# A hybrid retention and attention layer on one core: the attention's values become the stationary operand, two heads side by side in the array

## The chip, the cores and the metric

The kernel runs on one core of one Trainium2 chip. The metric is device time in microseconds (us) for one execution of the whole program, as the median of several runs; lower is better. Lines are cited as L361, meaning line 361 of the kernel before; where the changed kernel's own number differs, this is said.

## The reference

One layer over 256 tokens of width 1024, all in float32. The part that the change touches is the mixer:

```python
h = rmsnorm(x, mix_norm_g[l])
proj = h @ w_in[l]
rq, rk, rv, rg, mq, mk, mv, ga, gb = jnp.split(proj, offsets, axis=-1)
...
ret = retention(rq, rk, to_heads(rv, RET_HEADS))
y_a = (from_heads(ret) * jax.nn.silu(rg)) @ ret_w_branch[l]
att = moba_attention(mq, mk, to_heads(mv, MOBA_HEADS), rel_bias)
y_b = from_heads(att) @ moba_w_branch[l]
merged = jax.nn.sigmoid(ga) * y_a + jax.nn.sigmoid(gb) * y_b
x = x + merged @ w_out[l]
h2 = rmsnorm(x, ffn_norm_g[l])
x = x + peer(h2, peer_w_q[l], peer_sub_keys[l], peer_u[l], peer_v[l])
```

With 256 tokens there is one attention block, so the attention is plain causal attention over 8 heads of 64 with a relative-position bias that is added before the softmax. The retention has 8 heads with keys of 64 and values of 128, in two chunks of 128 tokens: the first chunk's keys and values give a state (64x128 for each head) that the second chunk's queries read. `peer` is a retrieval over 16,384 experts and takes the larger part of the time; the change does not touch it.

## The kernel before, in words

**The mixer as a row of pieces.** Every projection is cut into units of 512 columns, and every unit into pieces of 256 rows of the weight (512 KB each). The main loop runs over 72 mixer pieces. For piece i it issues a load some pieces ahead (`load_to`), splits the weight of piece i+3 into a high and a low part (`cut`: ScalarE writes the high part at L147, VectorE the low one at L148), and multiplies piece i (`products`, 12 matmuls of 512 columns at L230 to L232, or 24 of 256 columns at L239 to L241). The high parts (`rhi`), the low parts (`rlo`) and the products' PSUM tiles (`acc`) are rings.

**Side work between the pieces.** Everything else is written as Python generators (`attention`, `retention`, the epilogues of the units, `biases`). After each piece `pump` advances up to three of them to their next `yield`. What a generator emits between two yields is put behind that piece on every engine's queue, so a `yield` more means one piece more between two steps. The schedule is manual: each engine executes its instructions in the order in which the code emits them, and waits on semaphores where an operand is not ready.

**The bias table.** `biases` multiplies the bias by a one-hot table (L822), writes the rows to DRAM (`skew`, L825, GpSimd's queue), and some yields later reads them back, shifted, in 8 DMAs (L833, GpSimd's queue) into `bias`.

**The attention.** `attention` runs over two blocks t of 128 queries. Scores for two heads at a time come from matmuls on the two row halves of the array (64 rows each, L361). VectorE adds the bias (L365), takes the maximum (L369), ScalarE takes the exponent and the sums (L371, 8 heads), VectorE the reciprocal of the sums (L375). Then, for each block kt of 128 keys, TensorE turns the probabilities `pr` of 8 heads (L383), ScalarE copies them to `prT` (L384), and TensorE multiplies with `prT` as the stationary operand and 64 columns of the values `mv` as the moving one (L389). The result has queries in the partitions. VectorE multiplies it by the reciprocal (L393, into `at`), TensorE turns it (L400), and `split_to` splits it into `ah` and `al`, which a later projection (`branch_b`) reads. t = 0 has one block of keys, t = 1 has two.

**The retention.** The state `kv` comes from matmuls of 128 columns of `kdec` (two heads) by 256 columns of `rv` (L416), of which two quarters are used. Scores are L428, the output L441, the state's part L446.

**Rotary.** The epilogue of units 0 and 512 (`rotary`) has VectorE multiply into `ra` and `rb_` (L320, L322), GpSimd add them (L324) and scale (L330), and TensorE turn the result (L273).

**Order.** `finish(att)` runs what is left of the attention ahead of the unit at column 5632, since that unit's output `sb` takes the place of `bias` in memory.

Of the kernel before, what the change touches and what calls it, by code (L numbers as in the profile page):

```python
# [19 lines left out]
OP = mybir.AluOpType  # L20
# [55 lines left out]
def layer_kernel(ctx, tc, x, mix_norm_g, w_in, ret_w_branch, moba_q_gain, moba_k_gain, moba_w_branch,  # L76
# [273 lines left out]
    def attention():  # L350
        ssum = wk.tile([P, NT, H], F32, name="ssum")
        for t in range(NT):
            w = (t + 1) * P
            pr = wk.tile([P, H, S], F32, name="pr")
            nh = 512 // w
            for i0 in range(0, 4, nh):
                ps = [side() for _ in range(2)]
                for j in range(nh):
                    for c in range(2):
                        b = slice(c * 64, (c + 1) * 64)  # L360
                        T.matmul(ps[c][:, j * w:(j + 1) * w], mqk[0][b, i0 + j, t * P:(t + 1) * P],  # L361
                                 mqk[1][b, i0 + j, :w], start=True, stop=True)
                for c in range(2):
                    n = slice(4 * c + i0, 4 * c + i0 + nh)
                    V.tensor_tensor(pr[:, n, :w], ps[c].rearrange("p (j k) -> p j k", j=nh),  # L365
                                    bias[:, n, S - w:], op=OP.add)
                    yield
            sm = wk.tile([P, H], F32, name="smx")
            V.tensor_reduce(sm, pr[:, :, :w], axis=AX.X, op=OP.max, negate=True)  # L369
            for h in range(H):  # L370
                A.activation(pr[:, h, :w], pr[:, h, :w], AF.Exp, bias=sm[:, h:h + 1], accum_out=ssum[:, t, h:h + 1])  # L371
                if h % 4 == 3:
                    yield
            rs = wk.tile([P, H], F32, name="rs")
            V.reciprocal(rs, ssum[:, t, :])  # L375
            yield
            po = side()
            for kt in range(t + 1):
                prT = t4([P, H, P], "prT")
                for q in range(2):  # L380
                    p = side()
                    for j in range(4):
                        T.transpose(p[:, j * P:(j + 1) * P], pr[:, 4 * q + j, kt * P:(kt + 1) * P], ident)  # L383
                    A.activation(prT[:, 4 * q:4 * q + 4, :], p.rearrange("p (j i) -> p j i", j=4), AF.Copy)  # L384
                yield
                yield
                for i in range(H):
                    h = 2 * (i % 4) + i // 4
                    T.matmul(po[:, h * 64:(h + 1) * 64], prT[:, i, :], mv[:, kt, h * 64:(h + 1) * 64],  # L389
                             start=(kt == 0 and i == 0), stop=(kt == t), skip_group_check=True)  # L390
            at = t2([P, 512], "at")
            for c in range(2):
                V.tensor_tensor(at.rearrange("p (i c d) -> p c i d", c=2, d=64)[:, c],  # L393
                                po.rearrange("p (i c d) -> p c i d", c=2, d=64)[:, c],
                                rs[:, 4 * c:4 * c + 4, None].to_broadcast([P, 4, 64]), op=OP.mult)
            yield
            yield
            p = side()
            for c in range(4):
                T.transpose(p[:, c * P:(c + 1) * P], at[:, c * P:(c + 1) * P], ident)  # L400
            split_to(ah[0][:, :, t * P:(t + 1) * P], al[0][:, :, t * P:(t + 1) * P],
                     p.rearrange("p (c q) -> p c q", c=4))
            yield

    def mv_epi(o):
# [3 lines left out]
        yield  # L409

    def retention():
        for q in range(2):
            p = side()
            for j in range(2):
                hp = 2 * q + j
                T.matmul(p[:, j * S:(j + 1) * S], kdec[:, hp * P:(hp + 1) * P], rv[0][:, hp * S:(hp + 1) * S],  # L416
                         start=True, stop=True)
            A.activation(kv[:, 2 * q:2 * q + 2, :], p.rearrange("p (j e) -> p j e", j=2), AF.Copy)
            yield
        for t in range(NT):  # L420
            s = slice(t * P, (t + 1) * P)

# [20 lines left out]
            for j in range(4 if t else 0):  # L443
                for c in range(2):
                    b = slice(c * 64, (c + 1) * 64)
                    T.matmul(os_[c][:, j * P:(j + 1) * P], rqdT[b, j, :], kv[b, j, c * P:(c + 1) * P], start=False,  # L446
                             stop=True, skip_group_check=True)
            for c in range(2):
                for j in range(4):
# [54 lines left out]
    def merge_gate(dst, j):  # L504
        def epi(o):
            if j == 0:
                for t in range(NT):
                    A.activation(by_token(dst)[:, t], o[t], AF.Sigmoid)
                return
# [144 lines left out]
    sb = ap.tile([P, KC, S], F32, name="sb", tag="b8d")  # L654
    unit(w0, KC, 4608, hx, "nat", merge_gate(sa, 0))
    unit(w0, KC, 5120, hx, "T", merge_gate(sa, 1))
    unit(w0, KC, 5632, hx, "nat", merge_gate(sb, 0), before=lambda: finish(att))
    unit(w0, KC, 2048, hx, "nat", swish(0))
    unit(w0, KC, 2560, hx, "nat", swish(1))
    unit(w0, KC, 6144, hx, "T", merge_gate(sb, 1))  # L660
# [154 lines left out]
    def biases():  # L815
# [9 lines left out]
        G.dma_start(skew.rearrange("p h j -> h p j"), rr[:, None, :].to_broadcast([H, SK, 384]))  # L825
        yield
        V.tensor_scalar(gain[:, 0:1], gain[:, 0:1], 0.125, None, op0=OP.mult)
        for _ in range(5):
            yield

        s_ = skew[:, :, :]
# [605 lines left out]
```

## Time and profile before

| | |
|---|---|
| median of 3 runs | 948.59 us (946.0 to 951.2) |
| the profiled execution | 945.74 us, of which the span of the profile is 944.0 us |
| TensorE (PE) | busy 935.0 us, 99% of the span |
| VectorE (DVE) | busy 792.2 us, 84% |
| ScalarE (ACT) | busy 522.7 us, 55% |
| GpSimd (POOL) | busy 395.7 us, 42% |
| the mixer's stretch, 0 to 243 us | PE 240.96, DVE 168.55, ACT 127.13, POOL 34.53 us busy |
| DMA | 320.40 MB, mean 339 GB/s |

How to read the lines below: a line of the timeline gives the start in us, the duration in us, the engine, the line of the kernel, the operation, output<-input by the program's names, sizes, the count of instructions merged in it, and in brackets the idle time of the engine just before with what ended it. Matmuls are pipelined, so a matmul's duration overlaps its successor's, and what counts is the distance between two starts. A float32 matmul shows as two records.

### The profile page before, as it was taken

What the parts mean: (1) busy time and instruction counts of PE and PEld (TensorE: products, weight loads), DVE (VectorE), ACT (ScalarE), POOL (GpSimd) and SP (SyncE); (2) the same over time, 40 slices, a digit from 0 to 9 for tenths busy, and PEclk for the clock granted to TensorE, in tenths of its full rate; (3) what the DMA queues carried; (4) which work ended last, traced back from release to release, by engine and by line L of the source; (5) the groups of instructions that cost most, each with busy time, mean ns of one, the idle gap of its engine ahead of it and who ended that gap; (6) DMA issues with size and microseconds to landing.
All of it is one profiled execution on the core that took longest, in us unless ns stands there. A gap on an engine that the chain in (4) does not pass through costs nothing.

```text
span 944.0 us, 19147 instructions
## 1 busy us (share of the span) xinstructions
PE 935.0 (99%) x7208; PEld 896.5 (95%) x7208; DVE 792.2 (84%) x1514; ACT 522.7 (55%) x958; POOL 395.7 (42%) x306
## 2 busy tenths in 40 slices
PE   9999999999999999999999999999999999999998
PEld 6887898998999999999999999999999999999997
DVE  6657557778678999999988999974989999898987
ACT  6554645544544445434678777876454545364553
POOL 3422010000203446534556776763547656564720
PEclk9999999999999999999999999999999999999999
DMA  9878779998798998999999999998999999999993
GB/s 321 235 193 237 236 205 298 304 300 261 248 371 327 405 396 280 404 407 364 408 357 392 379 375 376 375 407 318 385 360 401 409 383 407 373 397 400 405 360 117
DMA packets 109419, 320.40 MB, mean 339 GB/s; under 512 B 11373, under 2 KB 22518, under 8 KB 109199
## 3 DMA queue, kind: packets, MB, share of 16 engines
q1 hardware_dynamic: 64492, 184.43, 54.8%
q0 software_dynamic: 32512, 115.54, 32.4%
q10 hardware_dynamic: 12322, 19.21, 6.8%
q8 instruction: 57, 0.93, 0.4%
q14 instruction: 36, 0.29, 0.1%
HBM read 307.52 MB, written 13.14 MB: 340 GB/s over the span
## 4 chain that ended last, share of the span: by engine, by line
PE 74%; DVE 15%; DMA 7%; ACT 1%; issue 1%; POOL 1%; SPq 0%; DVEq 0%; POOLq 0%; ACTq 0%
PE acc L1284 13%; PE acc L1316 9%; PE side L1316 9%; PE acc L230 6%; PE side L737 6%; PE acc L231 6%; PE acc L232 6%; PE acc L1317 4%; PE side L1317 4%; DVE rows L1044 3%; DMA raw_ring<-in_peer_w_q_dram 2%; PE acc L239 2%; PE acc L241 2%; PE acc L240 2%; PE side L1314 2%; PE acc L1314 2%
## 5 line engine op out<-in xcount | busy, mean ns | idle before, releaser
L1033 POOL DMA_INDIRECT rows<-in_peer_u_dram,eg x86 | 108.5, 1262 | 72.9 <-DVE rows L1044 34.0
L1033 POOL DMA_INDIRECT rows<-in_peer_v_dram,eg x54 | 100.2, 1856 | 67.1 <-DVE vacc L1119 45.7
L737 PE MATMUL side<-ident,raw_ring 128*128 128x128 f32 x800 | 107.2, 277 | 0.0
L737 PEld LDWEIGHTS side<-ident,raw_ring 128*128 128x128 f32 x800 | 97.0, 192 | 0.0
L1161 ACT ACTIVATE oh_buf<-oh_more,tS 128x128 bf16<-128x128 f16 x176 | 58.6, 420 | 0.0
L1044 DVE SCALAR_TENSOR_TENSOR rows<-rows,h 128x1024 f32<-128x1024 f32 x43 | 52.4, 1232 | 4.1 <-DMA rows<-in_peer_u_dram,eg 4.1
L1119 DVE SCALAR_TENSOR_TENSOR vacc<-rows,av,vacc 128x1024 f32<-128x1024 f32 x43 | 55.1, 1281 | 0.1
L1256 ACT ACTIVATE cw<-W 128x352 fp32r<-128x352 f32 x58 | 28.6, 494 | 47.6 <-PE acc L1317 38.5
L1242 POOL TENSOR_TENSOR W<-W,gl 128x256 f32<-128x256 f32 (+20 forms) x32 | 27.5, 861 | 46.3 <-ACT gl L1241 39.5
L1257 DVE TENSOR_TENSOR cw<-W,cw 128x352 fp32r<-128x352 f32 x58 | 30.3, 522 | 18.0 <-ACT cw L1256 18.0
L580 POOL DMA_DIRECT2D x1d<-xt x1 | 0.7, 657 | 88.5 <-DVE xt L562 88.5
L1156 DVE TENSOR_TENSOR oh_more<-iota,tI 128x1024 f16<-128x1024 f16 x44 | 34.5, 785 | 0.0
L1157 DVE TENSOR_TENSOR oh_buf<-oh_more,tM 128x1024 f16<-128x1024 f16 x44 | 32.6, 740 | 2.2
L154 POOL TENSOR_TENSOR gny<-va,minus_half 128x8 f32<-128x8 f32 x2 | 4.3, 2126 | 66.7 <-DVE va L454 66.7
L1284 PE MATMUL acc<-hTd,raw_ring 128*128 128x128 f32 x256 | 31.2, 275 | 0.0
L1284 PEld LDWEIGHTS acc<-hTd,raw_ring 128*128 128x128 f32 x256 | 29.9, 192 | 0.0
L1211 PE MATMUL acc<-oh_buf 128*128 128x128 bf16 x176 | 24.4, 219 | 0.0
L1212 PE MATMUL acc<-oh_buf 128*128 128x128 bf16 x176 | 24.4, 219 | 0.0
L1225 ACT ACTIVATE W<-acc 128x512 f32<-128x512 f32 (+21 forms) x44 | 17.3, 394 | 10.9 <-PE acc L1212 8.5
L1227 DVE TENSOR_TENSOR W<-acc,W 128x264 f32<-128x264 f32 (+20 forms) x32 | 16.1, 502 | 6.5 <-ACT W L1225 5.3
L1244 ACT ACTIVATE W<-acc 128x256 f32<-128x256 f32 (+20 forms) x52 | 18.4, 353 | 4.4 <-PE acc L1284 4.4
L1211 PEld LDWEIGHTS <-oh_buf 128*128 128x128 f16 x176 | 19.8, 114 | 0.0
(2701 smaller groups left out, 3486.4 us busy)
## 6 DMA issues: line engine op xcount, KB each, us to landing
raw_ring<-in_peer_v_dram SPq DMA_DIRECT2D x128, 512.0 KB
raw_ring<-in_peer_u_dram SPq DMA_DIRECT2D x100, 512.0 KB
raw_ring<-in_w_in_dram SPq DMA_DIRECT2D x52, 512.0 KB
raw_ring<-in_peer_w_q_dram SPq DMA_DIRECT2D x16, 512.0 KB
raw_ring<-turned SPq DMA_DIRECT2D x16, 512.0 KB
W<-in_peer_u_dram SPq DMA_DIRECT2D x12, 512.0 KB
eraw<-in_peer_u_dram ACTq DMA_DIRECT2D x32, 128.0 KB
h<-in_peer_u_dram ACTq DMA_DIRECT2D x32, 128.0 KB
```

What stands on the lines that cost most here:

```text
L230: T.matmul(o[t], xh[:, s], wh, start=(k == 0), stop=False)
L231: T.matmul(o[t], xh[:, s], wl, start=False, stop=False)
L232: T.matmul(o[t], xl[:, s], wh, start=False, stop=(k == kc - 1))
L737: T.transpose(p[:, k * P:(k + 1) * P], r.rearrange("p (i k) -> p k i", k=KC)[:, 4 * q + k], ident)
L1033: G.indirect_dma_start(out=r, out_offset=None, in_=tab, in_offset=bass.IndirectOffsetOnAxis(ap=eg[:, j:j + 1], axis=0))
L1044: V.scalar_tensor_tensor(r, r, 1.0, h, op0=OP.mult, op1=OP.mult, accum_out=av[:, j:j + 1])
L1119: V.scalar_tensor_tensor(a, r, av[:, j:j + 1], a, op0=OP.mult, op1=OP.add)
L1161: A.activation(o1[:, j], hot[:, 0, :, j], AF.Copy, scale=tS[:, t, k + j:k + j + 1])
L1211: T.matmul(p[:, j * P:(j + 1) * P], hi, o1, start=True, stop=False)
L1284: T.matmul(pa[:, n:n + NA], uT[:, k * P:(k + 1) * P], hT[:, k], start=(c % 2 == 0 and k == 0), stop=(k == KC - 1), skip_group_check=True)
L1316: T.matmul(o[b][:, :2 * ND], vh[:, n], w, start=(c == 0), stop=False, skip_group_check=True)
L1317: T.matmul(o[b][:, :ND], vl[:, n], w[:, :ND], start=False, stop=(c == NK - 1), skip_group_check=True)
```

## The change

The change has five parts.

1. **The product with the values.** The operands change places: 64 columns of `mv` are stationary and 128 columns of `prT` moving. A head's result is 64 partitions by 128 queries, and the two heads of a pair are written to partitions 0 to 63 and 64 to 127 of the same PSUM tile, from the two column halves of the array (L396 in the changed kernel; 8 matmuls for each block of keys as before). The result comes out turned, so the turn at L400 and `at` are gone, and `split_to` reads the product's tile.
2. **The division by the sums.** Since queries now lie in the free dimension of the result, VectorE multiplies `pr` by the reciprocal ahead of the turns (L378 in the changed kernel), in two instructions with a yield between them, in place of L393 behind the product.
3. **More pieces ahead of the turns.** Behind that come 1 + 2t yields, where one stood before. For t = 0 the turns stand one piece later than before, for t = 1 three.
4. **The retention's state** comes from 8 matmuls of 64 columns of `kdec` by 128 columns of `rv`, in the two column halves as well, in one PSUM tile instead of two.
5. **The order of the rest.** The bias table is read three yields sooner, and `finish(att)` moves from ahead of the unit at column 5632 to its epilogue.

```diff
             rs = wk.tile([P, H], F32, name="rs")
             V.reciprocal(rs, ssum[:, t, :])
-            yield
+            for c in range(2):
+                n = slice(4 * c, 4 * c + 4)
+                V.tensor_tensor(pr[:, n, :w], pr[:, n, :w], rs[:, n, None].to_broadcast([P, 4, w]), op=OP.mult)
+                if not c:
+                    yield
+            for _ in range(1 + 2 * t):
+                yield
             po = side()
...
-                for i in range(H):
-                    h = 2 * (i % 4) + i // 4
-                    T.matmul(po[:, h * 64:(h + 1) * 64], prT[:, i, :], mv[:, kt, h * 64:(h + 1) * 64],
-                             start=(kt == 0 and i == 0), stop=(kt == t), skip_group_check=True)
-            at = t2([P, 512], "at")
-            for c in range(2):
-                V.tensor_tensor(at.rearrange("p (i c d) -> p c i d", c=2, d=64)[:, c],
-                                po.rearrange("p (i c d) -> p c i d", c=2, d=64)[:, c],
-                                rs[:, 4 * c:4 * c + 4, None].to_broadcast([P, 4, 64]), op=OP.mult)
-            yield
-            yield
-            p = side()
-            for c in range(4):
-                T.transpose(p[:, c * P:(c + 1) * P], at[:, c * P:(c + 1) * P], ident)
+                for i in range(4):
+                    for c in range(2):
+                        h = 2 * i + c
+                        T.matmul(po[c * 64:(c + 1) * 64, i * P:(i + 1) * P], mv[:, kt, h * 64:(h + 1) * 64],
+                                 prT[:, 4 * c + i, :], start=(kt == 0 and i == 0), stop=(kt == t), skip_group_check=True)
+            yield
             split_to(ah[0][:, :, t * P:(t + 1) * P], al[0][:, :, t * P:(t + 1) * P],
-                     p.rearrange("p (c q) -> p c q", c=4))
+                     po.rearrange("p (c q) -> p c q", c=4))
             yield
...
     def retention():
-        for q in range(2):
-            p = side()
-            for j in range(2):
-                hp = 2 * q + j
-                T.matmul(p[:, j * S:(j + 1) * S], kdec[:, hp * P:(hp + 1) * P], rv[0][:, hp * S:(hp + 1) * S],
-                         start=True, stop=True)
-            A.activation(kv[:, 2 * q:2 * q + 2, :], p.rearrange("p (j e) -> p j e", j=2), AF.Copy)
-            yield
+        p = side()
+        for j in range(4):
+            for c in range(2):
+                n = j * P + c * 64
+                T.matmul(p[c * 64:(c + 1) * 64, j * P:(j + 1) * P], kdec[:, n:n + 64], rv[0][:, 2 * n:2 * n + P],
+                         start=(j == 0), stop=True, skip_group_check=True)
+        A.activation(kv[:, :, :P], p.rearrange("p (j e) -> p j e", j=4), AF.Copy)
+        yield
+        yield
...
-                    T.matmul(os_[c][:, j * P:(j + 1) * P], rqdT[b, j, :], kv[b, j, c * P:(c + 1) * P], start=False,
+                    T.matmul(os_[c][:, j * P:(j + 1) * P], rqdT[b, j, :], kv[b, j, :P], start=False,
...
             if j == 0:
+                if dst is sb:
+                    finish(att)
...
-    unit(w0, KC, 5632, hx, "nat", merge_gate(sb, 0), before=lambda: finish(att))
+    unit(w0, KC, 5632, hx, "nat", merge_gate(sb, 0))
...
-        for _ in range(5):
+        for _ in range(2):
             yield
```

Where this moves instructions is shown at three places. The first is VectorE's queue at t = 0, from the maximum `smx` on; `rlo__592` is the low part of piece 18, the rows with `ra` and `rb` are the rotary epilogue, and the next three `rlo` rows are pieces 19, 20 and 21. Before:

```order
L369 TENSOR_REDUCE smx<-pr 128x8
L148 TENSOR_TENSOR rlo__571<-raw_ring,rhi__570 128x1024
L148 TENSOR_TENSOR rlo__592<-raw_ring,rhi__591 128x1024
L320 TENSOR_TENSOR ra<-acc,rope 128x512
L322 TENSOR_TENSOR rb__608<-acc,rope 128x8x32 x2
L320 TENSOR_TENSOR ra<-acc,rope 128x512
L322 TENSOR_TENSOR rb__614<-acc,rope 128x8x32 x2
L375 RECIPROCAL rs<-ssum 128x8
L148 TENSOR_TENSOR rlo__625<-raw_ring,rhi__624 128x1024
L148 TENSOR_TENSOR rlo__658<-raw_ring,rhi__657 128x1024
L148 TENSOR_TENSOR rlo__679<-raw_ring,rhi__678 128x1024
L393 TENSOR_TENSOR at<-side,rs 128x4x64 x2
```

And now, from the reciprocal's predecessors on, with piece 19 named `rlo__626` and piece 20 `rlo__646`:

```order
L322 TENSOR_TENSOR rb__614<-acc,rope 128x8x32 x2
L375 RECIPROCAL rs<-ssum 128x8
L378 TENSOR_TENSOR pr<-pr,rs 128x4x128
L148 TENSOR_TENSOR rlo__626<-raw_ring,rhi__625 128x1024
L378 TENSOR_TENSOR pr<-pr,rs 128x4x128
L148 TENSOR_TENSOR rlo__646<-raw_ring,rhi__645 128x1024
```

The two multiplications of `pr` stand behind the rotary epilogue and the reciprocal, with the low part of piece 19 between them.

The second place is TensorE's queue at the turns of t = 0. Piece 16 is `rhi__547` with `rlo__548`, piece 17 `rhi__570` with `rlo__571`, piece 18 `rhi__591` with `rlo__592`. Before:

```order
L231 MATMUL acc<-rlo__548,hh 128x512
L232 MATMUL acc<-rhi__547,hl 128x512
L383 MATMUL side<-ident,pr 128x128 x8
L230 MATMUL acc<-rhi__570,hh 128x512
L231 MATMUL acc<-rlo__571,hh 128x512
```

And now:

```order
L231 MATMUL acc<-rlo__571,hh 128x512
L232 MATMUL acc<-rhi__570,hl 128x512
L389 MATMUL side<-ident,pr 128x128 x8
L230 MATMUL acc<-rhi__591,hh 128x512
L231 MATMUL acc<-rlo__592,hh 128x512
```

The turns (now at L389) went from behind piece 16 to behind piece 17. The first four of them read the heads of the first L378, the last four those of the second.

The third place is GpSimd's queue around the bias table; `qky` are the factors of the query and key norms, one instruction for each. Before:

```order
L825 DMA skew<-rr 8x16x384
L154 TENSOR_TENSOR qky<-qkss,minus_half 128x16 x2
L833 DMA bias<-skew 16x8x256 x8
L324 TENSOR_TENSOR ra<-ra,rb__608 128x512
L324 TENSOR_TENSOR ra<-ra,rb__614 128x512
```

And now:

```order
L826 DMA skew<-rr 8x16x384
L154 TENSOR_TENSOR qky<-qkss,minus_half 128x16
L834 DMA bias<-skew 16x8x256 x8
L154 TENSOR_TENSOR qky<-qkss,minus_half 128x16
L324 TENSOR_TENSOR ra<-ra,rb__608 128x512
L324 TENSOR_TENSOR ra<-ra,rb__614 128x512
```

The eight reads of the bias table went ahead of the second norm's factor.

## The prediction

> **What bounds the kernel now.** I read the page's busy times first, then TensorE's timeline through the mixer, then the waits of VectorE, GpSimd and ScalarE between 38 and 72 us. The page gives:
>
> ```profile
> span 944.0 us, 19147 instructions
> PE 935.0 (99%) x7208; PEld 896.5 (95%) x7208; DVE 792.2 (84%) x1514; ACT 522.7 (55%) x958; POOL 395.7 (42%) x306
> PE   9999999999999999999999999999999999999998
> ```
>
> TensorE is busy in every slice of the 40. A modelled busy share could hide pauses, so the distance between starts decides. TensorE's timeline around the first turns of `pr`:
>
> ```profile
> 58.36 0.39 PE L230 MATMUL acc<-rhi__547,hh 128*128 128x512 f32 x1
> 58.59 0.39 PE L231 MATMUL acc<-rlo__548,hh 128*128 128x512 f32 x1
> ...
> 61.09 1.19 PE L383 MATMUL side<-ident,pr 128*128 128x128 f32 x8
> 62.03 0.48 PE L230 MATMUL acc<-rhi__570,hh 128*128 128x512 f32 x1
> ```
>
> A matmul of 512 columns starts every 0.23 us, piece 16 (58.36 to 61.09) takes 2.73 us, and side work is inserted with nothing idle around it: the eight turns occupy 0.94 us. The row of slices says that it goes on so. The mixer is therefore as long as TensorE's list of instructions, and a microsecond taken off that list, or added to it as a wait, moves the end by a microsecond, since TensorE is just as full behind the mixer. VectorE's 7 us wait for the bias table costs nothing now:
>
> ```profile
> 53.04 0.69 DVE L365 TENSOR_TENSOR pr<-side,bias 128x512 f32<-128x512 f32 x1 [6.99 <-DMA bias<-skew]
> ```
>
> **The change part by part: TensorE's list.** The removed instructions, by distance between starts:
>
> ```profile
> 68.01 1.90 PE L389 MATMUL side<-mv,prT 128*128 128x64 f32 x16
> 69.72 0.48 PE L230 MATMUL acc<-rhi__624,hh 128*128 128x512 f32 x1
> 70.03 0.39 PE L231 MATMUL acc<-rlo__625,hh 128*128 128x512 f32 x1
> ...
> 76.18 0.60 PE L400 MATMUL side<-ident,at 128*128 128x128 f32 x4
> 76.54 0.47 PE L230 MATMUL acc<-rhi__678,hh 128*128 128x512 f32 x1
> ...
> 99.21 1.02 PE L416 MATMUL side<-rv,kdec 128*128 128x256 f32 x4
> 99.89 0.58 PE L230 MATMUL acc<-rhi__894,hh 128*128 128x512 f32 x1
> 100.30 0.40 PE L231 MATMUL acc<-rlo__895,hh 128*128 128x512 f32 x1
> ```
>
> The product with the values takes 1.71 us (68.01 to 69.72) and its follower 0.08 too much, 1.79 for each of three blocks of keys, 5.37 in all. The turn of `at` takes 0.36, twice, with one follower's 0.08: 0.80. The state takes 0.68 and its follower 0.18 too much, twice: 1.72. That is 7.89 us off.
>
> In their place come four groups of eight float32 matmuls on the two column halves. No column half is used in this trace; the nearest row is a group of eight on the two row halves, the next a group of eight on the whole array:
>
> ```profile
> 107.13 0.39 PE L232 MATMUL acc<-rhi__918,hl 128*128 128x512 f32 x1
> 107.45 1.16 PE L428 MATMUL side<-rqk,rqk 64*128 64x128 f32 x16
> 108.54 0.50 PE L230 MATMUL acc<-rhi__944,hh 128*128 128x512 f32 x1
> 108.88 0.39 PE L231 MATMUL acc<-rlo__945,hh 128*128 128x512 f32 x1
> ...
> 116.75 1.95 PE L441 MATMUL side<-rv,st 128*128 128x128 f32 x16
> 118.45 0.36 PE L239 MATMUL acc<-hh,rhi__1008 128*128 128x256 f32 x1
> ```
>
> On row halves the group takes 1.09 us, with 0.09 ahead (0.32 instead of 0.23) and 0.11 behind (0.34): 1.29. On the whole array, with the same 128 moving columns, it takes 1.70. So the four groups cost 4 x 1.29 = 5.16 if column halves overlap as row halves do, and 4 x (1.70 + 0.20) = 7.60 if they don't. The list becomes shorter by 2.7 us or by 0.3. I take 2.7: both are two halves of one array, with the same moving columns. The Trainium skill ("TensorE: Matmul & The Clock Gate", Part 3, on packing small matmuls by rows and columns) reports 2.38 times the speed for three column tiles, about as for row tiles; no run here shows it yet, and by it 2.7 stands.
>
> **The change part by part: when `pr` is ready.** The new multiplication L378 stands ahead of the turns on the path, where L393 stood behind the product. For t = 0 it decides. The steps that feed it, on VectorE, GpSimd and ScalarE:
>
> ```profile
> 47.35 0.50 PE L230 MATMUL acc<-rhi__448,hh 128*128 128x512 f32 x1
> ```
> ```profile
> 50.40 1.06 ACT L147 ACTIVATE rhi__547<-raw_ring 128x1024 fp32r<-128x1024 f32 x1 [2.35 <-PE acc L232]
> ```
> ```profile
> 56.51 1.21 DVE L369 TENSOR_REDUCE smx<-pr 128x8 f32<-128x1024 f32 x1
> 62.88 1.23 DVE L148 TENSOR_TENSOR rlo__592<-raw_ring,rhi__591 128x1024 fp32r<-128x1024 f32 x1 [1.26 <-ACT rhi__591 L147]
> 66.54 0.20 DVE L375 RECIPROCAL rs<-ssum 128x8 f32<-128x8 f32 x1
> 66.65 1.25 DVE L148 TENSOR_TENSOR rlo__625<-raw_ring,rhi__624 128x1024 fp32r<-128x1024 f32 x1
> 67.82 2.29 DVE L148 TENSOR_TENSOR rlo__658<-raw_ring,rhi__657 128x1024 fp32r<-128x1024 f32 x1
> 70.03 2.06 DVE L148 TENSOR_TENSOR rlo__679<-raw_ring,rhi__678 128x1024 fp32r<-128x1024 f32 x1
> ```
> ```profile
> 24.31 3.98 POOL L154 TENSOR_TENSOR qky<-qkss,minus_half 128x16 f32<-128x16 f32 x1 [3.04 <-DVE gain L827]
> 38.59 4.25 POOL L833 DMA_DIRECT2D bias<-skew  x8
> 65.52 1.29 POOL L324 TENSOR_TENSOR ra<-ra,rb__608 128x512 f32<-128x512 f32 x1 [22.68 <-DVE rb__608 L322]
> 66.77 2.25 POOL L324 TENSOR_TENSOR ra<-ra,rb__614 128x512 f32<-128x512 f32 x1
> 69.10 1.91 POOL L330 TENSOR_TENSOR rqd<-ra,col 128x512 f32<-128x512 f32 x1
> ```
>
> The table's eight reads took 4.25 us to issue, and VectorE could use it 10.2 us after the last (42.84 to 53.04). Now they follow the first `qky`, at 28.3, are issued by 32.5 and should be there by 42.7, before the scores end, ahead of the matmul at 47.35. The second `qky` now stands behind them; before, the reads at 38.59 followed it directly, so at some 4 us it began near 34.6, behind 32.5, and is not held. So the 7 us wait goes. What is late next is the high part of piece 16, `rhi__547`, which waits for TensorE until 50.40; its low part follows by 52.6, so the maximum starts at about 52.65, 3.86 us sooner than at 56.51. From there the distances between the rows hold: the reciprocal comes at 66.54 - 3.86 = 62.68 and is done at 62.9. Two L378 and one low part of a piece follow. A product of 128x512 from SBUF takes 0.63, by this row of two:
>
> ```profile
> 160.73 1.29 DVE L494 TENSOR_TENSOR ret<-ret,sg 128x512 f32<-128x512 f32 x2
> ```
>
> Alone they would end at 62.9 + 0.63 + 1.13 + 0.63 = 65.3. TensorE reaches the turns one piece later than before, at 61.09 + 2.73 = 63.82, and the second four, which need the second L378, at 64.26. It would wait 1.0 us.
>
> But they are not alone. GpSimd's rotary steps move with VectorE's: the second L324 comes at 66.77 - 3.86 = 62.91, just as the first L378 starts. The rows show what happens then: the first L324 took 1.29 us, the second 2.25, and it ended 1.2 after `rlo__625` (67.82); `rlo__658` took 2.29, ending 1.1 after that L324; L330 and `rlo__679` again took 1.91 and 2.06. They ran by turns, not side by side. By turns, L378 (0.63), L324 (1.25), `rlo__626` (1.13), L330 (1.2) and L378 (0.63) take 4.84 us in whatever order they begin: the second L378 ends at 62.9 + 4.84 = 67.75, and TensorE waits 3.5 us. The Trainium skill ("SBUF — State Buffer", summary of rules for kernel authors) says that when VectorE has two SBUF inputs while a GpSimd operation reads SBUF, the second to issue blocks until the first is done; the 2.29 beside 1.23 agrees, and it speaks against this change, as L378 reads two SBUF operands where L393 read one and PSUM. I take 3.5, as those rows are the same engines at the same step; the bounds are 0 and 3.5.
>
> Edits without a price: the t = 1 multiplications (two of 128x1024, 1.23 each by the `rlo` rows) come three pieces, 8.2 us, ahead of their turns, with GpSimd idle there; without that cover they would cost up to 2.5. `finish(att)` moves code that no one waits for: `ah` is first read at piece 52. The bias reads meet other weight loads than before, but `rhi__547` above waits for TensorE, not for its load, so the loads are ahead.
>
> Sum: 945.74 - 2.7 + 3.5 = 946.5 for the profiled execution, 0.8 us longer than before. That execution lies 2.85 us under the median of the runs; on the median it is 948.6 + 0.8 = 949.4.
>
> **The rivals.** First, GpSimd is not in the way: L378 has a broadcast operand, or the steps slide apart by a microsecond. For it: the reciprocal at 66.54, with one input, ran inside the first L324 and neither was slowed. The wait is 1.0 or nothing: 948.6 - 1.7 = 946.9, or 945.9.
>
> Second, the column halves don't overlap: 948.6 - 0.3 + 3.5 = 951.8. Against it: the row halves do.
>
> Third, on the slower side by most: the bias table comes no sooner, because the early reads share the DMA engines with the weight loads or stand behind the write of `skew`. Then the whole chain stays where it is, the reciprocal at 66.54, the second L378 at 71.6, and TensorE, now one step more dependent, waits 7.3 us: 948.6 - 2.7 + 7.3 = 953.2. There is slack: adding the bias must start by 52.65 - 3.47 = 49.2 (53.04 to 56.51 is 3.47), so it decides only once the table lands 6.5 us later than my 42.7; each microsecond beyond costs one.
>
> **How the numbers follow.** Forecast 0.50, first rival 0.28, second 0.13, third 0.09. All lie within 0.5% (4.7 us, about what a measurement of this kernel can tell from no change) of 948.6. The shown runs scatter by 2.6 us either way, so the first rival at 945.9 reaches below 943.9 in about 0.15 of its cases, with the others' tails 0.05 in all; the third rival at 953.2 exceeds 953.3 in half of its cases, with a fifth of the second's and some of the forecast's 0.08. The range runs from 945.9 less half the scatter, 944.5, to 952.3, half a microsecond above the second rival and short of the third.
>
> **What would show it.** Right: a pause of some 3.5 us on TensorE ahead of the second four turns at t = 0, L378 or `rlo__626` at double length beside L324, groups of column halves at 1.1 us, and no wait for `bias`. Wrong: groups at 1.7 us (second rival), turns without a pause (first), or VectorE still waiting for `bias` past 49 us (third). Pauses at other places of the mixer, or a mixer end that moves without the program's end moving, would make the whole reading wrong.

## The result and the profile after

The changed kernel takes 954.41 us (median of 8 runs, 952.98 to 957.66), the kernel before beside it 948.60 (8 runs, 945.65 to 951.20): a ratio of 1.0078, 95% interval 1.0061 to 1.0095. It is slower; the forecast was 949.4 us, and 954.4 lies outside its range. The profiled execution took 954.19 us with a span of 952.4.

The page of the changed kernel, beside that of before:

```profile
span 952.4 us, 19139 instructions
PE 936.8 (98%) x7208; PEld 895.8 (94%) x7208; DVE 796.1 (84%) x1514; ACT 522.2 (55%) x957; POOL 392.8 (41%) x306
PE   9989899999999999999899999999999999999998
PEclk9999899999999999999999999999999999999999
```

TensorE's row is no longer full: the slices at 48 to 71 us and 95 to 119 us show eights, and the clock has an eight in the fifth slice (the third eight of TensorE's row, at 452 us, lies behind the mixer). TensorE's waits, summed by what it waited for (total, times, longest), between 40 and 250 us; in the kernel before this view is empty:

```profile
PE side L389 <- DVE pr L378: 3.0, 1, 3.0
PE side L414 <- ACT rv L466: 2.6, 1, 2.6
PE side L389 <- ACT prT L390: 0.7, 1, 0.7
```

Three pauses. The first was forecast. The second stands at the retention's state, the third at t = 1; both were not.

**The first pause.** GpSimd's and VectorE's queues in the changed kernel, up to the second multiplication of `pr`:

```profile
63.55 1.81 POOL L324 TENSOR_TENSOR ra<-ra,rb__614 128x512 f32<-128x512 f32 x1
65.44 1.91 POOL L330 TENSOR_TENSOR rqd<-ra,col 128x512 f32<-128x512 f32 x1
```
```profile
48.09 0.69 DVE L365 TENSOR_TENSOR pr<-side,bias 128x512 f32<-128x512 f32 x1 [1.41 <-PE side L361]
...
63.31 0.19 DVE L375 RECIPROCAL rs<-ssum 128x8 f32<-128x8 f32 x1
63.54 0.69 DVE L378 TENSOR_TENSOR pr<-pr,rs 128x512 f32<-128x512 f32 x1
64.15 2.30 DVE L148 TENSOR_TENSOR rlo__626<-raw_ring,rhi__625 128x1024 fp32r<-128x1024 f32 x1
66.37 1.53 DVE L378 TENSOR_TENSOR pr<-pr,rs 128x512 f32<-128x512 f32 x1
```

VectorE no longer waits for the bias table but for the scores at 48.09; the table's eight reads were issued by 33.15 and landed 4.4 to 7.9 us after their issue. The low part of piece 19 and the second L378, beside the second L324 and L330, take 2.30 and 1.53 us where alone they take about 1.2 and 0.69. And TensorE:

```profile
64.44 0.60 PE L389 MATMUL side<-ident,pr 128*128 128x128 f32 x4
68.04 0.63 PE L389 MATMUL side<-ident,pr 128*128 128x128 f32 x4 [3.00 <-DVE pr L378]
...
68.82 0.63 PE L231 MATMUL acc<-rlo__592,hh 128*128 128x512 f32 x1
69.25 0.63 PE L232 MATMUL acc<-rhi__591,hl 128*128 128x512 f32 x1
```

Four turns take some 0.43, so the second four come 68.04 - 64.44 - 0.43 = 3.2 us late. Then comes something new: the products of 512 columns start 0.43 apart instead of 0.23. The changed kernel's windows give the reason in the column behind POOL, the granted clock (0.53 and 0.51 here):

```profile
68.40:71.80 3.40, 3.40 (x11) 2.67 (x10) 1.86 (x2) 1.54 (x2) 0.00 (x0) 0.53 0.75 245
...
106.00:112.80 6.80, 5.96 (x20) 4.59 (x21) 5.52 (x6) 2.81 (x5) 0.00 (x0) 0.51 0.82 240
```

Behind each of the two long pauses TensorE ran at half clock, once for 3.4 us and once for 6.8. In the kernel before the clock is 1.00 over the whole span. By distances between starts the first stretch costs 1.6 us (seven matmuls 0.20 too long each, 0.2 at the ends), the second 2.8 (0.47 in the state's second group, ten matmuls at 0.20, 0.37 at the ends).

**The second pause.** TensorE and ScalarE at the state, in the changed kernel:

```profile
103.59 0.66 PE L414 MATMUL side<-rv,kdec 128*64 128x128 f32 x8
106.84 1.12 PE L414 MATMUL side<-rv,kdec 128*64 128x128 f32 x8 [2.59 <-ACT rv L466]
```
```profile
100.36 0.51 ACT L371 ACTIVATE pr<-pr,smx 128x256 f32<-128x256 f32 x1 [3.71 <-DVE smx L369]
...
105.27 1.04 ACT L147 ACTIVATE rhi__938<-raw_ring 128x1024 fp32r<-128x1024 f32 x1
106.21 1.05 ACT L466 ACTIVATE rv<-acc 128x512 f32<-128x512 f32 x2
```

Heads 4 to 7 of the state read columns 512 and up of `rv`. ScalarE copies them (L466) behind t = 1's exponents and a high part, 2.6 us after TensorE has reached the matmuls that need them. In the kernel before the same copy stood just as late on ScalarE, but the state's second half stood one piece and eight turns later on TensorE:

```profile
96.07 0.51 ACT L371 ACTIVATE pr<-pr,smx 128x256 f32<-128x256 f32 x1 [3.70 <-DVE smx L369]
...
101.92 1.06 ACT L467 ACTIVATE rv<-acc 128x512 f32<-128x512 f32 x2
```
```profile
103.72 1.03 PE L416 MATMUL side<-rv,kdec 128*128 128x256 f32 x4
```

Of the two copies in the row the state reads the first, done at half of it, near 102.45, and TensorE came at 103.72, some 1.3 us later. Counted from the first exponent of t = 1 the copy stands alike in both kernels: it begins 5.85 us behind it (96.07 to 101.92, and 100.36 to 106.21). What moved is TensorE. The second half of the state started 4.51 us behind the first (99.21 to 103.72), with a piece and the eight turns of t = 1 between them; now it would start 0.59 behind it. That is 3.9 us sooner, and less the 1.3 us of slack it leaves the wait of 2.6. The `yield` between the two halves of the state, which the change took out, was this cover.

**What became shorter.** The first product with the values in the changed kernel:

```profile
76.58 1.09 PE L396 MATMUL side<-prT,mv 128*64 128x128 f32 x16
77.60 0.50 PE L230 MATMUL acc<-rhi__645,hh 128*128 128x512 f32 x1
```

1.02 us instead of 1.71. That is near the 1.09 of the row halves; whether it is the halves that overlap is tested below. With its edges (0.1 ahead and 0.1 behind, as in the forecast) a group costs about 1.2; the state's two groups of four, undisturbed (in the runs below), take 0.59 each. So the list became shorter by 7.89 - 3 x 1.2 - (2 x 0.59 + 0.2) = 2.9 us, where 2.7 was forecast.

**The sum.** One stretch of the program holds all of this, from the first product (`rhi__204`) to the first one of the mixer's last projection (`mh`). First the rows of before, then those of the changed kernel:

```profile
10.00 0.48 PE L230 MATMUL acc<-rhi__204,hh 128*128 128x512 f32 x1
217.08 0.40 PE L230 MATMUL acc<-rhi__2009,mh 128*128 128x512 f32 x1
```
```profile
10.63 0.47 PE L230 MATMUL acc<-rhi__204,hh 128*128 128x512 f32 x1
225.81 0.40 PE L230 MATMUL acc<-rhi__1999,mh 128*128 128x512 f32 x1
```

207.08 us before, 215.18 after: 8.1 longer. The parts are 3.2 and 2.7 us for the two pauses, 0.9 for the third, 4.4 at half clock, less 2.9: 8.3, 0.2 more than measured. Nearly all of it reaches the end: from there on the two executions take 726.9 and 726.6 us, and the span grew by 8.4.

### The profile page after: what moved, and what is told of

It is laid out like the page before. It is cut to its first block, busy times and chain, and to the rows that moved or that the text cites. A ratio compares the mean times of both kernels' runs of the same rounds, so it can differ in the third digit from the quotient of the medians.

```text
span 952.4 us, 19139 instructions
## 1 busy us (share of the span) xinstructions
PE 936.8 (98%) x7208; PEld 895.8 (94%) x7208; DVE 796.1 (84%) x1514; ACT 522.2 (55%) x957; POOL 392.8 (41%) x306
## 4 chain that ended last, share of the span: by engine, by line
PE 91%; DVE 4%; DMA 2%; ACT 1%; issue 1%; POOL 0%; ACTq 0%; SPq 0%; DVEq 0%; POOLq 0%
PE acc L1285 21%; PE side L738 10%; PE acc L1317 9%; PE side L1317 9%; PE acc L230 6%; PE acc L231 5%; PE acc L232 5%; PE acc L1318 4%; PE side L1318 4%; PE acc L240 3%; PE acc L239 3%; PE acc L241 3%; PE side L1315 2%; PE acc L1315 2%; DMA raw_ring<-in_peer_u_dram 1%; PE acc L1212 1%
## 5 line engine op out<-in xcount | busy, mean ns | idle before, releaser
L1034 POOL DMA_INDIRECT rows<-in_peer_v_dram,eg x54 | 96.7, 1791 | 73.6 <-DVE vacc L1120 57.1
```

The costliest lines, as they stand in the source:

```text
L1034: G.indirect_dma_start(out=r, out_offset=None, in_=tab, in_offset=bass.IndirectOffsetOnAxis(ap=eg[:, j:j + 1], axis=0))
```

## The experiments

All kernels ran beside the kernel before; ratios are to its time in the same batch. "Stretch" is the one just defined, from the profiled execution, with its difference from the 207.08 us of before. "Lost at half clock" is (1 - granted clock) x span, averaged over a kernel's runs; the kernel before loses 1.1 us by this count (35 runs beside the first four experiments, 1.0 to 1.3 beside the others; its profiled execution had a clock of 1.000). The clock of a run is given to 0.001, which is 0.95 us here, so single runs say little and averages more.

| kernel | median us | ratio [95%] | stretch, us | lost at half clock, us |
|---|---|---|---|---|
| changed | 954.41 | 1.0078 [1.0061, 1.0095] | +8.10 | 4.6 |
| turns later | 947.26 | 0.9998 [0.9974, 1.0022] | +3.55 | 2.4 |
| state split | 950.19 | 1.0022 [0.9998, 1.0047] | +2.91 | 1.9 |
| both mends | 943.89 | 0.9968 [0.9944, 0.9991] | -1.84 | 0.9 |
| pauses filled | 950.92 | 1.0045 [1.0019, 1.0072] | +3.88 | 1.1 |
| changed, again | 953.64 | 1.0066 [1.0045, 1.0088] | +3.73 | 4.1 |
| without GpSimd | 949.97 | 1.0039 [1.0017, 1.0061] | +3.83 | 3.4 |
| six turns in the pause | 948.50 | 1.0020 [0.9996, 1.0044] | +2.84 | 2.7 |
| thirteen turns | 949.69 | 1.0026 [1.0006, 1.0047] | +1.35 | 1.5 |
| bias sooner, alone | 946.63 | 0.9995 [0.9978, 1.0012] | -0.15 | 1.1 |
| late bias (11 runs) | 951.12 | 1.0055 [1.0033, 1.0077] | +2.73 | 4.2 |
| turns apart | 945.20 | 0.9976 [0.9952, 1.0001] | -0.19 | 1.7 |
| halves in turn | 945.27 | 0.9987 [0.9964, 1.0010] | -0.37 | 0.6 |

The theory: two pauses, each by a step that TensorE reaches before its operand is ready, and each followed by a stretch at half clock. The first rival: the clock fell for another reason (the column halves themselves, for instance), and the pauses would not matter so much. The second: the state's wait is not the missing piece.

### Turns a piece later

```diff
-            for _ in range(1 + 2 * t):
+            for _ in range(2 + t):
...
-            yield
+            if t:
+                yield
```

> The changed kernel, with the turns of t = 0 one piece later still (two yields instead of one behind the second L378), and the yield at the end of t = 0 taken out, so that t = 1 stays where it was. Theory W (two waits of TensorE, each followed by some 4 us of half clock): the pause ahead of the second four turns, 3.2 us, shrinks to under 0.5, with it the half clock behind it, 1.6: 4.4 to 4.8 us less than the changed kernel's 954.4, so about 949.8; the pause at the state's matmuls stays. Theory L (the longer time lies in the new list itself, in the column groups and what surrounds them, and a wait that is taken away turns up again at the next place): under 1.5 us less, above 952.9.

In this kernel the eight turns run together, 0.85 us to the next start, with no wait, and the clock is 1.00 there. The state's pause is as it was, and half clock follows it:

```profile
67.22 1.09 PE L389 MATMUL side<-ident,pr 128*128 128x128 f32 x8
```
```profile
98.47 0.66 PE L415 MATMUL side<-rv,kdec 128*64 128x128 f32 x8
101.71 1.12 PE L415 MATMUL side<-rv,kdec 128*64 128x128 f32 x8 [2.58 <-ACT rv L467]
```

The turns start 3.4 us later than in the changed kernel, counted from the first product: by the piece of 2.73, and by four turns of `ra` that now stand ahead of them. The second L378 ends at 67.54, just ahead of the second four turns (67.22 + 0.43 = 67.65). The stretch fell by 4.55 us, more than the pause: the half clock went with it. By the ratios the time fell by 0.0080, or 7.6 us, more than the 4.4 to 4.8 expected; each ratio is uncertain by 2 us or so, and the rest was not followed.

### The state in two groups, a piece apart

```diff
                          start=(j == 0), stop=True, skip_group_check=True)
+            if j == 1:
+                yield
         A.activation(kv[:, :, :P], p.rearrange("p (j e) -> p j e", j=4), AF.Copy)
         yield
-        yield
```

> The changed kernel, with the state's eight matmuls split in two groups of four, one piece apart, as before: the first reads the half of the retention's values that was copied long ago, the second the half that ScalarE copies late. Theory W: the 2.6 us pause inside the group goes, with the half clock behind it, 2.9: 5.3 to 5.6 us less than 954.4, about 949.0; the pause at the turns of t = 0 stays. Theory L: under 1.5 us less.

```profile
103.25 0.66 PE L414 MATMUL side<-rv,kdec 128*64 128x128 f32 x8
106.82 0.66 PE L414 MATMUL side<-rv,kdec 128*64 128x128 f32 x8
```

Neither group waits, and both take 0.59 us. The pause at the turns stays at 3.00. So the second pause comes from the missing piece between the two halves, and each pause goes without the other. The ratio fell by 0.0056, or 5.3 us, as expected.

### Both mends

> The changed kernel with both edits: turns of t = 0 one piece later, state in two groups. Theory W: the two gains add up, 9.7 to 10.4 us less than 954.4, about 944.3, which is below the kernel before (948.6) by what the shorter list is worth, 2 to 4 us, with one pause of 0.7 us left at the turns of t = 1. Theory L: no faster than the kernel before.

943.89 us: faster than the kernel before, by 0.0032 of its time with an interval of 0.0009 to 0.0056, and 1.84 us in the stretch. That is near the list's 2.9 less the third pause, which is still there (0.69 us, 0.9 by distances). In the stretch the two gains add up: 4.55 and 5.19 alone, 9.94 for both. What the change does to TensorE's list is a gain; its order lost it.

### Pauses filled

Twenty-six turns of the identity, which nobody reads, stand in the first pause and twenty-four in the second; pauses and half clock are told apart by adding work.

```diff
                     A.activation(prT[:, 4 * q:4 * q + 4, :], p.rearrange("p (j i) -> p j i", j=4), AF.Copy)
+                    if t == 0 and q == 0:
+                        fill = side()
+                        for _ in range(26):
+                            T.transpose(fill[:, :P], ident, ident)
...
+            if j == 1:
+                fill = side()
+                for _ in range(24):
+                    T.transpose(fill[:, :P], ident, ident)
```

> The changed kernel with work added where TensorE pauses: 26 turns of the identity between the two groups of four turns at t = 0 (2.8 us), and 24 between the fourth and fifth matmul pair of the state (2.6 us). Theory W: the operands arrive when they did, so the pauses end as before, but TensorE isn't idle in them and the granted clock stays at 1.00 behind them: 4 to 5 us less than 954.4, about 949.9, though 5.4 us of work are added. Rival C (the lower clock comes from something else, such as the column groups or the load at that place): the clock falls as before, and the time is 954.4 or more.

```profile
64.56 3.00 PE L394 MATMUL side<-ident 128*128 128x128 f32 x26
67.72 0.63 PE L389 MATMUL side<-ident,pr 128*128 128x128 f32 x4 [0.16 <-DVE pr L378]
```

The second four turns come as late as ever, but no matmul behind them is slow, and the stretch is 4.2 us shorter than in the changed kernel, with some 5.8 us of useless work in it. The ratio fell by 0.0033, or 3.1 us, a little less than the 4 to 5 expected. Over the ten runs 1.1 us were lost at half clock, no more than in the kernel before. The column halves are all in use here, so they don't lower the clock; the pauses do.

### The changed kernel again

> The changed kernel unaltered, timed beside the next three. Theory (each long pause of TensorE costs its own length and then some matmuls at half clock): both pauses, 3.0 to 3.2 us at the second four turns and 2.6 us at the state's second half, each followed by matmuls at 0.43 us instead of 0.23; ratio to before near 1.008. Rival (the first profile had a clock that was lowered for a reason of that execution): the pauses, but without the half clock, and a ratio near 1.003.

The ratio is as before, 1.0066, and its profiled execution parts the pauses from the clock:

```profile
67.53 0.63 PE L389 MATMUL side<-ident,pr 128*128 128x128 f32 x4 [3.00 <-DVE pr L378]
67.92 0.48 PE L230 MATMUL acc<-rhi__591,hh 128*128 128x512 f32 x1
...
104.77 0.66 PE L414 MATMUL side<-rv,kdec 128*64 128x128 f32 x8 [2.58 <-ACT rv L466]
105.35 0.50 PE L230 MATMUL acc<-rhi__888,hh 128*128 128x512 f32 x1
```

The same two pauses, and no half clock behind either (why is worked out at the end). The stretch is 3.73 us longer than before: 3.2 + 2.7 + 0.9 - 2.9 = 3.9, the three pauses less the shorter list. The rest of the first profile's 8.1 was the clock. In this execution the part behind the stretch took 732.8 us instead of 726.9 and brought the time back (955.49 us in all, the longest of the nine runs); of that some 1.5 us are a longer pause near 460 us (3.42, where the kernel before has 1.93), and about as much again is half clock behind it; the rest was not followed. Over all runs of the changed kernel the half clock cost 4.6 and 4.1 us in the two batches, over those of before 1.1: some 3 to 3.5 us of the loss.

### Without GpSimd's rotary steps

The two sums (L324) and the scaling (L330) of the first rotary epilogue are left out, so that the output lacks them; TensorE's list is the same.

> The changed kernel without GpSimd's work in the first rotary epilogue (two sums and the scaling; the sums and the scaling are left out of the output, TensorE's list is the same). By-turns theory (L378 and the low part of piece 19 were held by GpSimd's three instructions): the second L378 ends some 2 us sooner, L378 at about 0.65 and the low part at 1.2 us; TensorE's pause falls from 3.0 to about 1.0 us, and no half clock behind it; 3.5 us less than the changed kernel, ratio to before near 1.004. Rival (L378 is slow by itself, through its broadcast operand): it stays at 0.7 and 1.5 us, the pause stays near 3 us, ratio 1.008.

```profile
63.41 0.69 DVE L382 TENSOR_TENSOR pr<-pr,rs 128x512 f32<-128x512 f32 x1
64.02 1.22 DVE L148 TENSOR_TENSOR rlo__623<-raw_ring,rhi__622 128x1024 fp32r<-128x1024 f32 x1
65.15 0.69 DVE L382 TENSOR_TENSOR pr<-pr,rs 128x512 f32<-128x512 f32 x1
```
```profile
65.98 0.63 PE L393 MATMUL side<-ident,pr 128*128 128x128 f32 x4 [1.10 <-DVE pr L382]
```

1.22 and 0.69 us in place of 2.30 and 1.53, a wait of 1.10 in place of 3.00, no slow matmul behind it. The forecast gave TensorE a wait of 1.0 us with VectorE alone and of 3.5 beside GpSimd, so it is GpSimd's three steps that made the difference. The state's pause (2.61 us) stays in this kernel, and in the profiled execution half clock followed it for 3.4 us, which is why the stretch is no shorter than that of the changed kernel's second profile. The Trainium skill ("SBUF — State Buffer", summary of rules for kernel authors) has the second to issue blocked until the first is done, which these rows bear out.

### Part of the first pause filled

With the state split, so that the first pause stands alone, six and then thirteen turns of the identity stand in it.

> The changed kernel with the state in two groups of four a piece apart (no second pause) and six more turns of the identity between the first and the second four turns at t = 0: 0.7 us of work inside the 3.0 us pause, so the pause is about 2.3 us and the second L378 ends where it did. Theory of a limit between 2.3 and 2.6: no half clock, 1.6 us less than with the state split alone. Theory of a limit below 2.3: half clock as before, ratio as with the state split alone (1.002).

> As the one before, with thirteen turns of the identity: 1.5 us of work in the pause, about 1.5 us of pause left, the second L378 ends where it did. Theory of a limit (pauses above it cost some matmuls at half clock, those below it cost their length alone): no half clock if the limit lies above 1.5 us, and 1.6 us less than with the state split alone; half clock at full length if it lies below. Theory that the slow stretch is in proportion to the pause: half as many slow matmuls as behind 3 us, and 0.8 us less.

With six, then with thirteen:

```profile
67.59 1.09 PE L389 MATMUL side<-ident,pr 128*128 128x128 f32 x4 [2.38 <-DVE pr L378]
68.33 0.78 PE L230 MATMUL acc<-rhi__591,hh 128*128 128x512 f32 x1
68.90 0.63 PE L231 MATMUL acc<-rlo__592,hh 128*128 128x512 f32 x1
```
```profile
67.86 0.63 PE L389 MATMUL side<-ident,pr 128*128 128x128 f32 x4 [1.58 <-DVE pr L378]
68.24 0.47 PE L230 MATMUL acc<-rhi__591,hh 128*128 128x512 f32 x1
```

A pause of 2.38 us was still followed by half clock (matmuls 0.57 and 0.43 apart, where 0.31 and 0.24 are normal), one of 1.58 was not, and the stretch differs by 1.5 us although the second four turns come equally late. That looks like a limit between 1.6 and 2.4 us, but it isn't one. Over all runs 2.7 us were lost with six and 1.5 with thirteen, but only 1.9 with the state split alone, whose pause is the whole 3.0; the medians don't show the order either. And in other traces of this case a pause of 1.45 us was followed by half clock (at 12.66 us with the turns apart), while pauses of 2.42 (at 465.97 in the changed kernel) and 2.62 (at 457.97 with the turns apart) were not. The length alone doesn't decide; the last section shows what does.

### The bias table sooner, alone

One line of the change in the kernel before, `range(2)` for `range(5)`.

> The kernel before with one part of the change alone: the bias table read three yields sooner. Theory (VectorE's wait of 7 us for the table cost nothing, as TensorE never waited for it): VectorE's wait for the table goes, TensorE's list and spacing stay, ratio 1.000 within 0.0025. Rival (part of what the mended kernel gained comes from the earlier table and not from the column halves): ratio 0.997, like the kernel with both mends.

VectorE's wait for the table is gone, the reciprocal comes at 62.93 instead of 66.54, the stretch is 0.15 us shorter, and the ratio is 0.9995. A wait of 7 us on an engine that nobody waits for cost nothing.

### Both mends, but the table late

> The kernel with both mends (turns a piece later, state in two groups), but the bias table read as late as in the kernel before. Theory (the second L378 now decides when the turns can go, and it comes as late as the table lets it): the maximum near 56.5 and the reciprocal near 66.5 us, the second L378 ends near 71.6, TensorE pauses some 3.9 us ahead of the second four turns (67.6 without a wait), with half clock behind it in most runs; 5 us more than with both mends, ratio to before near 1.002. Rival (the early table is not needed once the turns stand a piece later): no pause, ratio 0.997.

```profile
53.08 0.69 DVE L365 TENSOR_TENSOR pr<-side,bias 128x512 f32<-128x512 f32 x1 [6.16 <-DMA bias<-skew]
...
66.60 0.19 DVE L375 RECIPROCAL rs<-ssum 128x8 f32<-128x8 f32 x1
```
```profile
71.32 0.63 PE L389 MATMUL side<-ident,pr 128*128 128x128 f32 x4 [2.88 <-DVE pr L378]
```

The same line matters here: the chain is back at 66.60, the pause is back (2.88 us, where 3.9 was expected), and the half clock with it. The stretch grew by 4.6 us against both mends. The ratio of 1.0055 is more than the 1.002 expected, and its interval begins at 1.0033. Part of what is missing is half clock behind the mixer, 3.4 us of it near 460 us in the profiled execution; the rest was not followed. One of the twelve executions took 4985.37 us and is in none of these figures; why was not followed either.

### At t = 1 the turns apart

The kernel with both mends, with a `yield` between the first and the second four turns of the second block of keys.

> The kernel with both mends, and at t = 1 a piece between the first and the second four turns of the second block of keys, where TensorE waited 0.69 us for a free PSUM tile. Theory (each pause left costs its length, and this one is too short to lower the clock): the wait goes, 0.7 to 0.9 us less than with both mends, ratio to before 0.996. Rival: the pause moves to the product with the values, which now stands one piece later, and the time stays, ratio 0.997.

The wait of 0.69 us is gone. The time is unclear: 0.9976, with an interval that holds the 0.9968 of both mends. The profiled execution has a pause of 1.45 us near its start (0.2 to 0.6 in the other runs that show it), where TensorE waits for the low part of the first piece, and half clock for 3.4 us behind it (0.91 on the mean of the first 20 us, 1.8 us lost). Without these some 2.9 us its stretch would be about 1.2 us shorter than that of both mends, an estimate from one execution. So the wait is gone, but this kernel is not shown to be faster than both mends.

### One column half after the other

The kernel with both mends, with the two loops of the product with the values exchanged.

> The kernel with both mends, with the loops of the product with the values exchanged: first the four heads of one column half, then the four of the other, in place of one half after the other by turns; the instructions are the same. Theory (the time saved comes from two neighbours on different column halves running at once): each of the three groups takes near 1.7 us instead of 1.02, with only one pair at the change of halves overlapping, 1.8 us more in all, ratio to before near 0.999. Rival (a matmul with 64 columns stationary is short by itself): the groups stay at 1.02 us and the ratio at 0.997.

```profile
120.95 1.58 PE L396 MATMUL side<-prT,mv 128*64 128x128 f32 x16
122.46 0.66 PE L389 MATMUL side<-ident,pr 128*128 128x128 f32 x4
```

The same instructions take 1.51 us in place of 1.02, three times, and the stretch is 1.47 us longer: it is neighbours on different halves that overlap. 1.51 is below the 1.7 expected, so a small part of the gain comes without the alternation. The medians (0.9987 and 0.9968) don't part by their intervals.

## Why the prediction was wrong

**Right: the list.** 2.7 us were forecast, 2.9 are read, and with both mends the stretch is 1.84 us shorter with 0.9 still lost in the third pause. The choice of the row halves as the nearest row held (1.09 us there, 1.02 here), and the loops exchanged show why.

**Right: the first pause.** 3.5 us of waiting were forecast, by turns of VectorE and GpSimd; 3.0 came (3.2 by distances), and 1.1 without GpSimd (1.0 was forecast). The chain ahead of it was right too: counted from the first product, the maximum starts at 42.65 us and the reciprocal at 52.68, which is just what the forecast's 52.65 and 62.68 come to, less the 10.00 of the first product in the trace of before. The bias table came with time to spare.

**Wrong: the state.** The working on TensorE's list has "The state takes 0.68 and its follower 0.18 too much, twice: 1.72", and prices its new form by its length alone. The change also took out the piece between the two halves, and the forecast never asked when the second half's operand is ready, though it asked just that of `pr`. In the trace of before the answer stood 1.3 us apart: the copy of `rv` is done near 102.45, the matmuls come at 103.72. With the piece and the eight turns between the two halves gone from in front of them, they came 3.9 us sooner against ScalarE and had to wait 2.6. The pause cost 2.7 us by distances, and the split state took it away. The sum had this wait at nothing. The text itself named "pauses at other places of the mixer" as what would make the reading wrong.

**Wrong: what a pause costs.** "A microsecond taken off that list, or added to it as a wait, moves the end by a microsecond" holds for the list and fails for waits of this length. Behind seven of the nine pauses of 2.4 to 3.0 us that the mixers of these kernels show, the granted clock fell to 0.5 for 3.4 or 6.8 us. The two stretches cost 4.4 us in the first profile and some 3 to 3.5 on the average of the runs. With the clock at 1.00, as in the second profile, the same kernel lost only the pauses.

**Wrong: a small one.** The edits "without a price" looked at L378 at t = 1, but not at the PSUM tiles of the turns three pieces later. TensorE waited 0.69 us there until ScalarE had copied the first four (0.9 by distances). The turns a piece apart removed it; why a tile is free in the kernel before and not here was not tried.

Put together: -2.9 + 3.2 was forecast nearly right, and 2.7 + 0.9 + some 3 to 3.5 us of half clock were not in the sum. That makes 6.9 to 7.4 us; 0.0078 and 0.0066 of 948.6 are 7.4 and 6.3. Of the rivals, none had this mechanism: the two on the slower side put the loss into the list and into the bias table, and the runs speak against both.

## What to carry to other kernels

When a change merges two groups of instructions, look up for each operand when it is ready and how much the piece that goes was covering: here 1.3 us of slack stood in the trace, against a step of 3.9. On an engine that is otherwise always busy, count a pause of two and a half to three microseconds at about one and a half times its length (5.9 us of pauses here, and 3 to 3.5 of half clock), and look at the granted clock behind it. If a shorter list brings a longer time, mend the order before giving up the list: both moves of one piece together turned 1.0078 into 0.9968.

## What the hardware showed beyond expectation

TensorE's clock falls to half for 3.4 us (68.62 to 72.04 in the changed kernel) or twice that (106.16 to 113.00, and 101.00 to 107.82 with the turns later). It does so now in the pause, now up to 1.6 us behind it (104.86 without GpSimd, where the pause ended at 103.24). Which pauses are followed is no matter of their length alone: over all traces a pause of 1.45 us was followed, and so was one of 1.82 (at 456.77, with the bias sooner alone), while 3.00 and 2.58 of the changed kernel's second profile, 2.62 and 2.42 were not.

The traces show what decides. All changes of the clock in one execution lie on a grid of 3.413 us: in the changed kernel the three later ones of the four times above lie 1, 11 and 13 steps behind the first, and with the late bias the changes at 75.94, 461.64 and 465.06 lie 1, 114 and 115 steps behind that at 72.52. Ten traces have such a change, so that their grid is known. In these, leaving out the last 15 us of the program, the clock fell at the end of every step in which TensorE had been idle for 1.67 us or more (eleven steps, 1.67 to 2.99), and at the end of no step with less (the most is 1.65). This idle time is the step less PE's busy time, whose ends are modelled, and one fall in the last 3 us of a program came behind 1.57; so the border is about half a step, known to some 0.1 us. Where the next step still held 0.7 us of the pause, as at the state, the half clock lasted two steps.

| execution | step | idle in it, us | clock behind it |
|---|---|---|---|
| changed, first pause | 65.21 to 68.62 | 2.83 | half |
| changed, again, first pause | 62.78 to 66.19 | 1.65 | full |
| the same | 66.19 to 69.61 | 1.34 | full |
| turns apart, at its start | 9.85 to 13.26 | 1.67 | half |

So the luck is in where a pause meets the grid. The pause of 3.00 us in the second profile was cut in two by the grid, neither part long enough. By these two numbers, a step of 3.41 and a border of 1.67, a pause of 2.6 us in a place of its own is followed in about eight of ten positions, one of 3.0 in nine, and one below some 1.5 in none: an estimate, in which the grid stands anywhere with equal chance. It fits that the 1.58 us of thirteen turns were not followed; the 1.45 at the start of the turns apart was followed only since the same step held more idle time.

The Trainium skill ("TensorE: Matmul & The Clock Gate", Part 1, "What's actually happening") describes a free-running window of 3.4 us, and a clock that goes to half after an idle one. The grid and the lengths here, one or two of 3.4, agree with it. That a whole window must be idle doesn't: here 1.67 us of a window were enough, and the measured pauses decide.
